# Sixteen column tiles of a mixer's input projection as 2x2 block products in a stage of their own, their results through DRAM

## The chip, the cores and the metric

The kernel runs on one core of one Trainium2 chip. The metric is the time of one execution on the device in microseconds (us). Three runs of the kernel before took 2117.59, 2117.65 and 2117.67 us; one more run was profiled, and all rows of the trace come from that one. PE is TensorE, DVE VectorE, ACT ScalarE, POOL GpSimd, and SP the engine that only issues DMAs.

## What is computed

One encoder layer for 1024 tokens of width 1024: a SwiGLU feed-forward (FFN) half step, a mixer, a second FFN half step, with a layer norm after each. Only the mixer's code changes. Its core in the reference is:

```python
proj = h @ w_in        # 1024 x 5152
na_q, na_k, na_v, g_q, g_k, g_v, g_g, dlf, dlb, gate_na, gate_gla = split(proj)
y_na  = neighborhood_attention(na_q, na_k, na_v, na_rpb) @ w_branch_na
y_gla = gla_bidirectional(g_q, g_k, g_v, g_g, dlf, dlb, ...) @ w_branch_gla
merged = sigmoid(gate_na) * y_na + sigmoid(gate_gla) * y_gla
return merged @ w_out
```

NA is neighbourhood attention with 8 heads of 64 columns on a grid of 16 rows by 64 columns; GLA is gated linear attention with 4 heads, in both directions, with silu(g_g) as its output gate. The kernel keeps float32 accuracy: every operand is split into a rounded high part and the remainder as low part (`split`, `load_w`), and each product of 128x128 weights with 512 tokens is three matmuls (high x high, high x low, low x high). Activations stand with the 1024 columns as 8 tiles `k` of 128 partitions, in two halves `h` of 512 tokens.

## The kernel before, in words

PE's instructions run in the order of the program text (`tc.manual_schedule(engines={PE})`); a scheduler orders the other engines, each of which then runs its own list strictly in order. `run` draws from generators that issue PE's dense matmuls; each step of three adds 0.65 to a clock (`STEP`). `at(t, f)` puts an event on that clock: when the dense work has come to `t`, `f` issues its instructions between two steps. `flush` issues what is left.

The stages, in order: the first FFN (`one.go`), the values of NA (`tok_major(wnv)`, stored to DRAM as `vscr`), the NA stage, the GLA stage, the merge, the output projection with its norm, the second FFN.

The FFNs compute two column tiles at a time as a 2x2 block product, seven block products in place of eight (Strassen's scheme, Winograd's form): `sums_of` makes the four sums of activation blocks (`T`), `factors` the four sums of weight blocks, `product` issues one block product (4 tiles x 3 matmuls = 12 matmuls), `blocks` strings them together.

The mixer before takes no part in that: each column tile is loaded by `load_w` and multiplied by `mm_steps`, 48 matmuls for both halves.

- NA stage (L1016 to L1026). `qk_pair(p)` computes the q and k tiles of two heads (96 matmuls), with q's moving operand read in the order of attention blocks (`blk`), and splits them from PSUM into the attention's operands on ACT and DVE (L928 to L936). Its 16 small loads `vp<-vscr` (L916) go over SP's queue. Sixteen attention events per pair run between the matmuls of the next pair: event i issues the scores of block i (2 matmuls), the transposes of block i-2 (3) and, in every second event, the values of two blocks (12). Between scores and transposes of a block stand DVE's bias add and minimum (L966), ACT's exponential (L968), DVE's reciprocal and scaling (L970, L971). `spill` computes the four tiles of GLA's q and k and stores them; `decay_rank` and `tok_major(wgv)` follow.
- GLA stage (L1223 to L1235). `gate_na(j)` computes a gate tile, its sigmoid and the NA branch's projection; `out_gate(i)` computes a tile of the output gate (48 matmuls), its silu and the product with the GLA output, which `gla_otrans` had put into DRAM (`gos`). GLA's own work is placed by `GLA_T0`, `GLA_DT` and `GLA_OUT`.
- Merge (L1243). `merge(j)` loads two weight tiles, computes a gate tile (48 matmuls), its sigmoid, the GLA branch's projection (24 matmuls), and combines both branches; then `project` multiplies by `w_out`.

Of the kernel before, what the change touches and what calls it, by code (L numbers as in the profile page):

```python
# [8 lines left out]
F32 = mybir.dt.float32  # L9
F32R = mybir.dt.float32r  # L10
# [8 lines left out]
P = 128  # L19
# [19 lines left out]
GLA_D0 = 6.0  # L39
GLA_T0 = 27.5  # L40
GLA_DT = 31.1
GLA_NEXT = 8.5
GLA_OUT = (15.0, 29.0, 29.0, 37.0)
NA_T0 = 3.3
FIRST = (1, 2, 4, 8)
# [19 lines left out]
def hybrid_layer(ctx, tc, xT, wg1, wu1, wds1, wd1, wg2, wu2, wds2, wd2, wcol, wnv, wgv, wdl, wgate,  # L65
# [362 lines left out]
    class Ffn:  # L428
# [133 lines left out]
        def blocks(self, fs):  # L562
# [4 lines left out]
            for f in [*fs, None]:  # L567
                if f is not None:
                    w = self.factors(f)
                    X = dps()  # L570
# [248 lines left out]
    one = Ffn(ffn1, x, xr, half(xT), wg1, wu1, wds1, wd1, 0)  # L819
    one.go(first, ((0, 0, HF), (1, 0, HF)), lambda h, c0, cn: to_x(x1, h))  # L820

# [4 lines left out]
    gos = dram.tile([4, P, S], F32, tag="gos", name="gos")  # L826
    m1s = dram.tile([KD, P, S], F32, tag="m1s", name="m1s")

    dls = dram.tile([32, S], F32, tag="dls", name="dls")


    def tok_major(w_d, dst, alloc=None):
        wq = []
        for i in range(4):
            if alloc is None:
                wh, wl = load_w(w_d[i], D)
                wq += [(wh[:, :HF], wl[:, :HF]), (wh[:, HF:], wl[:, HF:])]
                continue
            raw = wpool.tile([P, D], F32, tag="raw", name=nm("raw"), bufs=2)
# [19 lines left out]

    def spill(src, m, dst, scale=1.0):  # L860
        w = load_w(src, KD * m)
        for h in range(2):
            ps = dps((m, HF))
            yield from mm_steps(ps, w, x1h[h])
            sb = stage()
            nc.scalar.activation(sb[:m], ps, AF.Copy, scale=scale)
            nc.sync.dma_start(dst[:, h * HF:(h + 1) * HF], sb[:m])

    run(tok_major(wnv, lambda t: vscr[t * P:(t + 1) * P, :], one.hpair))
    assert not pending  # L870
    ffn1.close()
    x1h = [[x1[k][h] for k in range(KD)] for h in range(2)]

    def decay_rank():
# [5 lines left out]
        for h in range(2):  # L880
# [13 lines left out]
            nc.sync.dma_start(dls[:, h * HF:(h + 1) * HF], sb[0:32])  # L894

    vgrid = vscr.rearrange("(r c) e -> r c e", c=64)
    nap = ExitStack()
# [7 lines left out]
    def qk_pair(p):  # L905
        wq = load_w(wcol[p], D)
        wk = load_w(wcol[4 + p], D)
        k2 = [npool.tile([P, S], F32R, tag="k2", name=nm("k2"), bufs=4) for _ in range(2)]
# [3 lines left out]
        pair[p] = (q2, k2, kl, vp)  # L912
        for b in range(4):
            w = COLW[b]
            for g in range(4):
                nc.sync.dma_start(vp[:4 * w, 4 * b + g, :],  # L916
                                  vgrid[4 * g:4 * g + 4, COL0[b]:COL0[b] + w, p * P:(p + 1) * P])
        for h in range(2):
            hs = slice(h * HF, (h + 1) * HF)
            pq = dps()  # L920
            yield from mm_steps(pq, wq, [(blk(hi), blk(lo)) for hi, lo in x1h[h]])
            sides = []
            for hh in range(2):
                a, o = slice(64 * hh, 64 * hh + 64), slice(64 - 64 * hh, 128 - 64 * hh)
                t = npool.tile([P, HF], F32R, tag="q2", name=nm("q2"), bufs=4)
                q2[hh][h] = t
                sides.append((hh, a, o))
                nc.scalar.activation(t[a], pq[a], AF.Copy, scale=0.125)  # L928
                nc.vector.scalar_tensor_tensor(t[o], pq[a], 0.125, t[a].bitcast(F32),
                                               ALU.mult, ALU.subtract)  # L930
            pk = dps()
            yield from mm_steps(pk, wk, x1h[h])
            for hh, a, o in sides:
                nc.scalar.activation(k2[hh][a, hs], pk[a], AF.Copy)
                nc.vector.tensor_copy(k2[hh][o, hs], pk[a])
                nc.vector.tensor_tensor(kl[a, hs], pk[a], k2[hh][a, hs].bitcast(F32),  # L936
                                        ALU.subtract)


# [75 lines left out]

    run(qk_pair(0))  # L1016
    gl = [spill(wcol[8 + i], P, gqk[i], 0.125 if i < 2 else 1.0) for i in range(4)]
    na_events(0, 16, NA_T0, 41)
    run(gl[0], decay_rank(), qk_pair(1))
    na_events(16, 32, NA_T0, 41)  # L1020
    run(gl[1], gl[2], qk_pair(2))
    na_events(32, 48, NA_T0, 31)
    run(gl[3], qk_pair(3))
    na_events(48, 67, NA_T0, 41)
    run(tok_major(wgv, lambda t: gv[t]))
    flush()  # L1026
# [25 lines left out]
    for h, tag in enumerate(("on", "gst")):  # L1052
        hs = slice(h * HF, (h + 1) * HF)
        dlr = gp.tile([32, HF], F32, tag=tag, name=nm("dlr"))
        nc.sync.dma_start(dlr, dls[:, hs])
# [9 lines left out]
    def gla_decay(hd):  # L1065
# [6 lines left out]
        v = gp.tile([P, 8, P], F32, tag="gvt", name=nm("gvt"))  # L1072
        nc.sync.dma_start(v, gv[:, :, hd * P:(hd + 1) * P].rearrange("t p e -> p t e"))
# [108 lines left out]
    def gla_otrans(hd, h):  # L1182
        on = heads[hd]["on"]
        pt = aux.tile([P, HF], F32, tag="pt", name=nm("opt"), bufs=1)
        for t in range(4):
            nc.tensor.transpose(pt[:, t * P:(t + 1) * P], on[:, t], ident)
        sb = gp.tile([P, HF], F32, tag="gst", name=nm("gst"))
        nc.scalar.activation(sb, pt, AF.Copy, scale=ngt[:, 0:1])
        nc.sync.dma_start(gos[hd, :, h * HF:(h + 1) * HF], sb)

# [15 lines left out]
    def out_gate(i):  # L1206
        w = load_w(wcol[12 + i], D)
        for h in range(2):
            ps = dps()
            yield from mm_steps(ps, w, x1h[h])  # L1210
            og_in = lp.tile([P, HF], F32, tag="hr", name=nm("ld"), bufs=1)
            nc.sync.dma_start(og_in, gos[i, :, h * HF:(h + 1) * HF])
            sb = stage()
            nc.scalar.activation(sb, ps, AF.Silu)
            nc.vector.tensor_tensor(sb, sb, og_in, ALU.mult)
            hi, lo = atile(F32R), atile(F32R)
            split(sb, hi, lo)
            og[i][h] = (hi, lo)

    at(GLA_D0, lambda: gla_decay(0))  # L1220
    for hd in range(4):
# [10 lines left out]
        for i, t in enumerate(GLA_OUT):  # L1232
            add(t, (gla_out, gla_otrans)[i % 2], hd, i // 2)
    run(*[gate_na(j) for j in range(KD)], *[out_gate(i) for i in range(4)])
    assert not pending  # L1235
    gla.close()
# [6 lines left out]
    def merge(j):  # L1243
        wga = load_w(wgate[KD + j], D)
        wb = load_w(wbr[1, j], HF)
        for h in range(2):
            m1 = lp.tile([P, HF], F32, tag="hr", name=nm("ld"), bufs=1)
            nc.sync.dma_start(m1, m1s[j, :, h * HF:(h + 1) * HF])
            pg = dps()
            yield from mm_steps(pg, wga, x1h[h])  # L1250
            sb = stage()
            nc.scalar.activation(sb, pg, AF.Sigmoid)
            py = dps()
# [8 lines left out]
    def project(d, h, sink):  # L1262
# [133 lines left out]
```

## Time and profile before

| | |
|---|---|
| median of three runs | 2117.65 us |
| the profiled execution | 2116.91 us |
| its span, first to last instruction | 2115.1 us |
| mean granted clock of PE | 0.998 |
| PE busy | 2091.7 us, 99% of the span, 9818 matmuls |
| DVE, ACT, POOL busy | 1327.8, 866.7, 90.8 us |
| HBM traffic | 199.91 MB read, 82.97 MB written |

The profile is that of one core. A matmul of 512 columns is listed with a duration of some 390 ns, but the next one starts before it ends: the price of a matmul is the distance from its start to the next start, which a timeline shows, and not its listed duration. "Busy" is the union of the durations, so an engine that is busy 99% may still have waits hidden in long durations. "SPq" rows are SP's DMA issues. The chain that ended last puts 93% of the span on PE.

### The profile page before, as it was taken

How to read it: one execution, taken by the hardware profiler on the slowest of the kernel's cores; microseconds unless marked ns; L12 is line 12 of the kernel's file. 1: busy time of each engine (PE TensorE's matmuls, PEld its weight loads, DVE VectorE, ACT ScalarE, POOL GpSimd, SP SyncE). 2: the span in 40 equal slices, each digit the busy share in tenths (PEclk: the TensorE clock that was granted, in tenths of full speed). 3: DMA queues.
4: the chain of work that ended last, by engine and by line, in shares of the span. 5: the costliest groups of instructions: out<-in, count | busy, mean ns of one | idle time of the engine just before them, and what ended most of it. 6: DMA issues, size and time to landing. Idle time of an engine off the chain costs nothing.

```text
span 2115.1 us, 26389 instructions
## 1 busy us (share of the span) xinstructions
PE 2091.7 (99%) x9818; PEld 1705.1 (81%) x9818; DVE 1327.8 (63%) x2270; ACT 866.7 (41%) x1439; POOL 90.8 (4%) x86
## 2 busy tenths in 40 slices
PE   9999999999999999999999999999999999999997
PEld 7888888888887867777888888877888888888887
DVE  8667776456668244543777433499776776557647
ACT  6444444312234244445566422245544444322222
POOL 0000000000014100000000000034000000000001
PEclk9999999999999999999999999999999999999999
DMA  4444443496631223223334222221343443396722
GB/s 146 152 142 150 166 162 110 142 327 218 224 115 43 93 78 99 89 61 100 92 108 122 91 85 80 95 81 69 111 178 126 168 151 134 125 318 215 239 100 80
DMA packets 145409, 284.63 MB, mean 135 GB/s; under 512 B 15264, under 2 KB 39584, under 8 KB 145280
## 3 DMA queue, kind: packets, MB, share of 16 engines
q1 hardware_dynamic: 145280, 282.94, 39.9%
q8 instruction: 77, 1.26, 0.2%
q14 instruction: 52, 0.43, 0.1%
HBM read 199.91 MB, written 82.97 MB: 134 GB/s over the span
## 4 chain that ended last, share of the span: by engine, by line
PE 93%; DVE 4%; POOL 1%; DMA 1%; issue 1%; ACT 0%; SPq 0%; DVEq 0%; POOLq 0%; ACTq 0%
PE d L556 15%; PE d L558 15%; PE d L557 15%; PE d L119 9%; PE d L121 9%; PE d L120 9%; PE d L658 3%; PE d L657 3%; PE d L656 3%; PE d L852 1%; PE d L854 1%; PE d L853 1%; PE po L997 1%; PE pt L979 1%; PE s L962 1%
## 5 line engine op out<-in xcount | busy, mean ns | idle before, releaser
L119 PE MATMUL d<-xh,wh 128*128 128x512 f32 x640 | 259.1, 405 | 0.1
L120 PE MATMUL d<-xl,wh 128*128 128x512 f32 x640 | 251.3, 393 | 1.0 <-POOL xl L409 0.5
L121 PE MATMUL d<-xh,wl 128*128 128x512 f32 x640 | 251.2, 393 | 0.5 <-DVE wl L109 0.5
L128 ACT ACTIVATE wh<-raw 128x512 fp32r<-128x512 f32 (+4 forms) x132 | 98.0, 753 | 173.2 <-PE d L557 70.2
L129 DVE TENSOR_TENSOR wl<-raw,wh 128x512 fp32r<-128x512 f32 (+4 forms) x132 | 109.9, 841 | 88.2 <-ACT wh L128 88.1
L678 DVE TENSOR_TENSOR a<-a,d 128x512 f32<-128x512 f32 (+1 forms) x152 | 100.0, 658 | 90.1 <-PE d L558 60.0
L119 PEld LDWEIGHTS d<-xh,wh 128*128 128x128 f32 x640 | 120.3, 188 | 32.8 <-issue 4.5
L121 PEld LDWEIGHTS d<-xh,wl 128*128 128x128 f32 x640 | 120.3, 188 | 27.0 <-DVE wl L109 1.0
L120 PEld LDWEIGHTS d<-xl,wh 128*128 128x128 f32 x640 | 120.5, 188 | 26.6 <-DVE xl L129 2.0
L108 ACT ACTIVATE wh<-raw 128x512 fp32r<-128x512 f32 (+1 forms) x91 | 82.5, 907 | 136.0 <-PE d L120 80.0
L109 DVE TENSOR_TENSOR wl<-raw,wh 128x512 fp32r<-128x512 f32 (+1 forms) x91 | 96.1, 1057 | 62.9 <-ACT wh L108 62.1
L656 PE MATMUL d<-hh,wh 128*128 128x512 f32 (+1 forms) x368 | 134.5, 365 | 0.0
L658 PE MATMUL d<-hh,wl 128*128 128x512 f32 (+1 forms) x368 | 133.2, 362 | 0.0
L657 PE MATMUL d<-hl,wh 128*128 128x512 f32 (+1 forms) x368 | 133.2, 362 | 0.0
L556 PE MATMUL d<-a,wh 128*128 128x512 f32 x320 | 124.9, 390 | 1.6 <-DVE hr L584 1.6
L558 PE MATMUL d<-xh,wl 128*128 128x512 f32 x320 | 124.8, 390 | 0.4 <-DVE wl L129 0.4
L557 PE MATMUL d<-a,wh 128*128 128x512 f32 x320 | 124.7, 390 | 0.0
L558 PE MATMUL d<-a,wl 128*128 128x512 f32 x320 | 124.7, 390 | 0.0
L558 PE MATMUL d<-hh,hl 128*128 128x512 f32 x320 | 124.7, 390 | 0.0
L556 PE MATMUL d<-xh,wh 128*128 128x512 f32 x320 | 124.7, 390 | 0.0
L556 PE MATMUL d<-hh,hh 128*128 128x512 f32 x320 | 124.7, 390 | 0.0
L557 PE MATMUL d<-xl,wh 128*128 128x512 f32 x320 | 124.7, 390 | 0.0
(309 smaller groups left out, 4690.0 us busy)
## 6 DMA issues: line engine op xcount, KB each, us to landing
raw<-in_wu SPq DMA_DIRECT2D x44, 512.0 KB
raw<-in_wg SPq DMA_DIRECT2D x43, 512.0 KB
ops<-oh SPq DMA_DIRECT2D x84, 256.0 KB
ops<-ol SPq DMA_DIRECT2D x84, 256.0 KB
oh<-ops SPq DMA_DIRECT2D x48, 256.0 KB
ol<-ops SPq DMA_DIRECT2D x48, 256.0 KB
hid<-oh SPq DMA_DIRECT2D x40, 256.0 KB
hid<-ol SPq DMA_DIRECT2D x40, 256.0 KB
```

The lines of the kernel that those rows point to most:

```text
L119: nc.tensor.matmul(ps, a, xh, start=k == 0, stop=False)
L120: nc.tensor.matmul(ps, a, xl, start=False, stop=False)
L121: nc.tensor.matmul(ps, wl[:, k * m:(k + 1) * m], xh, start=False, stop=k == n - 1)
L128: nc.scalar.activation(hi, src, AF.Copy)
L129: nc.vector.tensor_tensor(lo, src, hi.bitcast(F32), ALU.subtract)
L556: nc.tensor.matmul(ps, a, xh, start=first and k == 0, stop=False, **sg)
L557: nc.tensor.matmul(ps, a, xl, start=False, stop=False, **sg)
L558: nc.tensor.matmul(ps, wl[:, k * P:(k + 1) * P], xh, start=False, stop=k == n - 1, **sg)
L656: nc.tensor.matmul(ps, wh, hi, start=k == 0, stop=False)
L657: nc.tensor.matmul(ps, wh, lo, start=False, stop=False)
L658: nc.tensor.matmul(ps, wl, hi, start=False, stop=k == n - 1)
L678: nc.vector.tensor_tensor(a, a, ps, ALU.add)
```

## The change

- Sixteen column tiles (NA's q and k, GLA's q and k, the output gate) are taken out of their places and computed as eight pairs in a new stage `pairs`, between `decay_rank` and the NA stage, with the FFN's `factors` and `product` and new `sums_of`. Each pair is 7 block products of 12 matmuls. For this the first norm's outputs are kept (`x1r`) until `sums_of` has read them.
- The results go to DRAM over GpSimd's queue (`qks`, `gqk`, `ogs`; 32 stores of 256 KB). `qk_pair` no longer multiplies: it reads q and k back over GpSimd's queue and splits them from SBUF; its 16 `vp` loads move from SP's to GpSimd's queue too, behind the first q and k loads.
- NA's 64 events now run in one go from 13.0 on the clock, 1.05 apart, between `tok_major(wgv)` and four gate tiles `gate_gla(4..7)`; before, 2.36, 2.36, 1.73 and 1.98 apart.
- `wgv`'s weights are loaded during the last pair (`last()`).
- `gate_gla(j)` computes the gate tiles of the merge earlier and stores them unsigmoided to `gts`; 1, 2 and 3 follow `gate_na`, 0 stands just ahead of the merge. `merge` loads them and applies the sigmoid.
- `gla_otrans` multiplies by the gate that `gla_out` loads from `ogs`; `out_gate` only loads and splits. The last head's output stays in SBUF.

```diff
-NA_T0 = 3.3
+NA_T0 = 13.0
+NA_DT = 1.05
+NA_GATES = (4, 5, 6, 7)
+GLA_GATES = (1, 2, 3)
...
+    def pairs(mb, items, last):
+        x, T = mb.x, mb.T
+        b11, b21, b22 = ([x[k + o][h] for k in range(4)] for o, h in ((0, 0), (4, 0), (4, 1)))
+
+        def store(out, h, t, src=None):
+            dst, fn, scale = out
+            if src is not None or fn != AF.Copy or scale != 1.0:
+                nc.scalar.activation(t, t if src is None else src, fn, scale=scale)
+            nc.gpsimd.dma_start(dst[:, h * HF:(h + 1) * HF], t)
...
+                w = mb.factors(wcol[it[0]], wcol[it[1]])
+                if it is items[-1]:
+                    last()
+                X = dps()
+                yield from mb.product(X, w["a11"], b11, True)
...
+            if prev:
+                yield from mb.product(pX, pw["a22"], T[3])
+                with hoist():
+                    store(g[3], 0, mb.tmp(), pX)
...
+    for i in range(4):
+        one.sums_of(i)
+    run(decay_rank())
...
+    run(pairs(one, [(p, 4 + p, plain(qks[p], 0.125), plain(qks[4 + p])) for p in range(4)]
+              + [(8, 9, plain(gqk[0], 0.125), plain(gqk[1], 0.125)),
+                 (10, 11, plain(gqk[2]), plain(gqk[3]))]
+              + [(12 + i, 13 + i, (ogs[i], AF.Silu, 1.0), (ogs[i + 1], AF.Silu, 1.0))
+                 for i in (0, 2)], lambda: wq.extend(tok_weights(wgv, 4))))
...
     def qk_pair(p):
-        wq = load_w(wcol[p], D)
-        wk = load_w(wcol[4 + p], D)
...
-            pq = dps()
-            yield from mm_steps(pq, wq, [(blk(hi), blk(lo)) for hi, lo in x1h[h]])
...
+            pq, pk = (npool.tile([P, HF], F32, tag="qr", name=nm("qr"), bufs=3)
+                      for _ in range(2))
+            nc.gpsimd.dma_start(pq, qks[p, :, hs])
+            nc.gpsimd.dma_start(pk, qks[4 + p, :, hs])
...
+                nc.scalar.activation(t4[a], q4[a], AF.Copy)
+                nc.vector.tensor_tensor(t4[o], q4[a], t4[a].bitcast(F32), ALU.subtract)
                 nc.scalar.activation(k2[hh][a, hs], pk[a], AF.Copy)
                 nc.vector.tensor_copy(k2[hh][o, hs], pk[a])
                 nc.vector.tensor_tensor(kl[a, hs], pk[a], k2[hh][a, hs].bitcast(F32),
                                         ALU.subtract)
+        for b in range(4):
+            w = COLW[b]
+            for g in range(4):
+                nc.gpsimd.dma_start(vp[:4 * w, 4 * b + g, :],
+                                  vgrid[4 * g:4 * g + 4, COL0[b]:COL0[b] + w, p * P:(p + 1) * P])
...
+    qk_pair(0)
+    for p in range(1, 4):
+        at(NA_T0 + (16 * p - 13) * NA_DT, lambda p=p: qk_pair(p))
+    na_events(0, 67, NA_T0, NA_T0 + 67 * NA_DT)
+    run(tok_major(wgv, lambda t: gv[t], wq=wq), *[gate_gla(j) for j in NA_GATES])
...
     def merge(j):
-        wga = load_w(wgate[KD + j], D)
...
+            m1, sb = (mp.tile([P, HF], F32, tag=t, name=nm(t), bufs=3) for t in ("m1", "sb"))
+            nc.sync.dma_start(m1, m1s[j, :, hs])
+            nc.sync.dma_start(sb, gts[j, :, hs])
+            nc.scalar.activation(sb, sb, AF.Sigmoid)
```

Before, SP's queue holds these rows where the loads for NA's first two pairs stand (`vp_6026` belongs to pair 0, `vp_6380` to pair 1; `bt` are bias tiles, `raw` weights):

```order
L916 DMA vp_6026<-vscr 128x1x128 x5
L916 DMA vp_6026<-vscr 96x1x128 x4
L952 DMA bt_6192<-in_bias 128x2x288
L952 DMA bt_6243<-in_bias 128x768
L916 DMA vp_6380<-vscr 96x1x128 x4
L916 DMA vp_6380<-vscr 128x1x128 x8
L916 DMA vp_6380<-vscr 96x1x128 x4
L107 DMA raw_6699<-in_wcol 128x1024
```

Now GpSimd's queue holds, from the last stores of the new stage on (L888), the loads of pair 0 (`qr_7282` to `qr_7299`, `vp_7281`) and then those of pair 1 (`qr_7459` and on, `vp_7458`):

```order
L888 DMA ogs<-hr_7271 128x512
L990 DMA qr_7282<-qks 128x512
L991 DMA qr_7283<-qks 128x512
L990 DMA qr_7298<-qks 128x512
L1007 DMA vp_7281<-vscr 96x1x128 x4
L1007 DMA vp_7281<-vscr 128x1x128 x2
L991 DMA qr_7299<-qks 128x512
L1007 DMA vp_7281<-vscr 128x1x128 x6
L1007 DMA vp_7281<-vscr 96x1x128 x4
L990 DMA qr_7459<-qks 128x512
L991 DMA qr_7460<-qks 128x512
L990 DMA qr_7475<-qks 128x512
```

The loads of a pair, 20 in all, now stand behind the stage's last store and behind those of the pair before, in one list; pair 1's rest and the first of pair 2 follow in the same way.

On DVE, before, pair 1's k is split from PSUM (`d_6489`) between the attention's own instructions (`e`, `sm`; `kl` and `k` are the split's results):

```order
L966 ISA e_6547,sm_6548<-s_6544,bt_6542 128x384
L966 ISA sm_6548 128x1
L935 CAST k_1310_6377<-d_6489 64x512
L970 RECIPROCAL sm_6548<-sm_6548 128x1
L936 TENSOR_TENSOR kl_6379<-d_6489,k_1310_6377 64x512
L971 TENSOR_SCALAR e_6547<-e_6547,sm_6548 128x384
L935 CAST k_1311_6378<-d_6489 64x512
L936 TENSOR_TENSOR kl_6379<-d_6489,k_1311_6378 64x512
```

Now pair 1's q and k are split from the tiles that GpSimd's queue loads (`qr_7459`, `qr_7460`, `qr_7475`), right behind the minimum of event 2 (`e_7442`) and ahead of its scaling:

```order
L1037 ISA e_7442,sm_7443<-s_7439,bt_7437 128x384
L1037 ISA sm_7443 128x1
L999 TENSOR_TENSOR q_1680_7463<-qr_7459,q_1680_7463 64x8x4x16
L1001 CAST k_1674_7455<-qr_7460 64x512
L1002 TENSOR_TENSOR kl_7457<-qr_7460,k_1674_7455 64x512
L1041 RECIPROCAL sm_7443<-sm_7443 128x1
L1001 CAST k_1675_7456<-qr_7460 64x512
L1042 TENSOR_SCALAR e_7442<-e_7442,sm_7443 128x384
L999 TENSOR_TENSOR q_1681_7469<-qr_7459,q_1681_7469 64x8x4x16
L1002 TENSOR_TENSOR kl_7457<-qr_7460,k_1675_7456 64x512
L999 TENSOR_TENSOR q_1684_7479<-qr_7475,q_1684_7479 64x8x4x16
L999 TENSOR_TENSOR q_1685_7485<-qr_7475,q_1685_7485 64x8x4x16
```

The split's first row there waits for a DMA now, where it waited for PE, and the attention rows behind it wait with it. The first row of pair 2's split stands in the same manner behind the minimum of event 6.

More of the change, by code (lines that the diff above doesn't have):

```diff
@@ L819, in hybrid_layer, with to_x1, sink @@
     one = Ffn(ffn1, x, xr, half(xT), wg1, wu1, wds1, wd1, 0)
-    one.go(first, ((0, 0, HF), (1, 0, HF)), lambda h, c0, cn: to_x(x1, h))
+    x1r = [[None, None] for _ in range(KD)]
+    def to_x1(h, c0, cn):
+        put = to_x(x1, h)
+        def sink(d, y):
+            put(d, y)
+            x1r[d][h] = y
+        return sink
+    one.go(first, ((0, 0, HF), (1, 0, HF)), to_x1)
     vscr = dram.tile([S, HF], F32, tag="vscr", name="vscr")
@@ L858, in tok_major @@
             nc.sync.dma_start(dst(t), sb)
[L860 to L871, printed above, removed]
@@ L872, in hybrid_layer @@
-    x1h = [[x1[k][h] for k in range(KD)] for h in range(2)]
+    def pairs(mb, items, last):
[6 more added lines that the diff above has]
+            nc.gpsimd.dma_start(dst[:, h * HF:(h + 1) * HF], t)
+        prev = None
+        for it in [*items, None]:
+            if it:
+                w = mb.factors(wcol[it[0]], wcol[it[1]])
[3 more added lines that the diff above has]
+                yield from mb.product(X, w["a11"], b11, True)
+                s1 = mb.tmp()
+                with hoist():
+                    nc.scalar.activation(s1, X, AF.Copy)
+                Y = dps()
+                yield from mb.product(Y, w["a12"], b21, True)
+                with hoist():
+                    nc.vector.tensor_tensor(s1, Y, s1, ALU.add)
+                store(it[2], 0, s1)
+            if prev:
+                g, pX, p5, pw = prev
+                yield from mb.product(pX, pw["s3"], T[2])
+                with hoist():
+                    nc.vector.tensor_tensor(p5, pX, p5, ALU.add)
+                store(g[3], 1, p5)
+            if it:
+                Z = dps()
+                yield from mb.product(Z, w["s1"], T[0], True)
+                s5 = mb.tmp()
+                with hoist():
+                    nc.scalar.activation(s5, Z, AF.Copy)
+                yield from mb.product(X, w["s2"], T[1])
+                s2 = mb.tmp()
+                with hoist():
+                    nc.scalar.activation(s2, X, AF.Copy)
+            if prev:
+                yield from mb.product(pX, pw["a22"], T[3])
+                with hoist():
+                    store(g[3], 0, mb.tmp(), pX)
+            if it:
+                yield from mb.product(Z, w["s4"], b22)
+                with hoist():
+                    nc.vector.tensor_tensor(s2, Z, s2, ALU.add)
+                store(it[2], 1, s2)
+                prev = it, X, s5, w
@@ L894, in decay_rank @@
             nc.sync.dma_start(dls[:, h * HF:(h + 1) * HF], sb[0:32])
+    run(tok_major(wnv, lambda t: vscr[t * P:(t + 1) * P, :], one.hpair))
+    assert not pending
+    x1h = [[x1[k][h] for k in range(KD)] for h in range(2)]
+    one.x, one.xr = x1, x1r
+    for i in range(4):
+        one.sums_of(i)
+    run(decay_rank())
+    plain = lambda t, scale=1.0: (t, AF.Copy, scale)
+    wq = []
+    run(pairs(one, [(p, 4 + p, plain(qks[p], 0.125), plain(qks[4 + p])) for p in range(4)]
[3 more added lines that the diff above has]
+                 for i in (0, 2)], lambda: wq.extend(tok_weights(wgv, 4))))
+    ffn1.close()
     vgrid = vscr.rearrange("(r c) e -> r c e", c=64)
@@ L1014, in na_events, with gate_gla @@
                 at(t, lambda i=s: na_scores(i))
[L1016 to L1025, printed above, removed]
+    def gate_gla(j):
+        w = load_w(wgate[KD + j], D)
+        for h in range(2):
+            ps = dps()
+            yield from mm_steps(ps, w, x1h[h])
+            sb = stage()
+            nc.scalar.activation(sb, ps, AF.Copy)
+            nc.sync.dma_start(gts[j, :, h * HF:(h + 1) * HF], sb)
+    qk_pair(0)
[3 more added lines that the diff above has]
+    run(tok_major(wgv, lambda t: gv[t], wq=wq), *[gate_gla(j) for j in NA_GATES])
     flush()
@@ L1206, in out_gate @@
     def out_gate(i):
-        w = load_w(wcol[12 + i], D)
         for h in range(2):
[L1209 to L1212, printed above, removed]
             sb = stage()
[L1214 to L1218, printed above, removed]
+            nc.sync.dma_start(sb, gos[i, :, h * HF:(h + 1) * HF])
+            og[i][h] = atile(F32R), atile(F32R)
+            split(sb, *og[i][h])
     at(GLA_D0, lambda: gla_decay(0))
@@ L1233, in hybrid_layer @@
             add(t, (gla_out, gla_otrans)[i % 2], hd, i // 2)
-    run(*[gate_na(j) for j in range(KD)], *[out_gate(i) for i in range(4)])
-    assert not pending
+    run(*[gate_na(j) for j in range(KD)])
+    for i in range(3):
+        at(4.0 * i, lambda i=i: out_gate(i))
+    run(*[gate_gla(j) for j in GLA_GATES])
+    flush()
     gla.close()
@@ L1271, in project @@
         sink.add(a)
+    run(gate_gla(0))
     for j in range(KD):
```

72 lines of the change are left out of this document (34 added, 38 removed).

## Prediction, made before the change was run

> **What bounds the kernel now.** I read the page first: PE is busy almost throughout.
>
> ```profile
> span 2115.1 us, 26389 instructions
> PE 2091.7 (99%) x9818; PEld 1705.1 (81%) x9818; DVE 1327.8 (63%) x2270; ACT 866.7 (41%) x1439; POOL 90.8 (4%) x86
> PE 93%; DVE 4%; POOL 1%; DMA 1%; issue 1%; ACT 0%; SPq 0%; DVEq 0%; POOLq 0%; ACTq 0%
> ```
>
> The chain in the third line says the same: 93% of the span is PE's own work, so a matmul taken away is time gained unless something else comes late in its place. What a matmul costs is read from stretches, by windows (us, then busy time and number per engine). The first is the twenty blocks of the first FFN, the second the mixer up to the merge, the third the 64 attention events, the fourth a part of the merge stage, the last the stretch just ahead of the mixer's tiles.
>
> ```profile
> 53.20:434.90 381.70, 380.92 (x1681) 315.25 (x1680) 247.49 (x377) 170.48 (x275) 0.00 (x0) 1.00 0.44 152
> 710.40:1345.40 635.00, 635.00 (x3241) 500.27 (x3241) 317.84 (x626) 286.16 (x480) 3.56 (x13) 1.00 0.30 92
> 737.00:990.00 253.00, 253.00 (x1382) 184.10 (x1380) 114.31 (x316) 114.09 (x255) 1.96 (x5) 1.00 0.25 79
> 1222.00:1345.00 123.00, 123.00 (x545) 101.91 (x544) 45.00 (x60) 31.32 (x46) 0.00 (x0) 1.00 0.26 82
> ...
> 690.00:710.00 20.00, 20.00 (x90) 16.55 (x90) 0.00 (x0) 3.56 (x7) 3.10 (x3) 1.00 0.17 66
> ```
>
> 381.7 us for 1681 matmuls is 0.227 us each, without a hole: a block product of 12 costs 2.72 us, a pair of column tiles done in blocks 84 x 0.227 = 19.1 us. The merge stage runs at the same pace (123.0/545 = 0.226). The granted clock is 1.00 throughout. In the mixer (second row) PE never stood still for 635 us; the other engines have half the time free, and that slack is what the change spends.
>
> **The matmuls removed.** Sixteen tiles of 48 matmuls are 768, eight pairs of 84 are 672: 96 fewer, 96 x 0.227 = 21.8 us. PE's list confirms the number, 9122 rows against 9218. The q tiles were dearer than that, because their moving operand was read in blocks; the timeline shows the first q product, the first k product and the next q product starting at
>
> ```profile
> 710.44 0.40 PE L119 MATMUL d<-xh,wh 128*128 128x512 f32 x1
> ...
> 716.18 0.40 PE L119 MATMUL d<-xh,wh 128*128 128x512 f32 x1
> ...
> 721.67 0.40 PE L119 MATMUL d<-xh,wh 128*128 128x512 f32 x1
> ```
>
> 5.74 us for q's 24 matmuls, 5.49 for k's. Eight q products in plain order save another 8 x 0.27 = 2.2 us. The attention's own matmuls, the gates and both branch projections stay the same in number. So 24.0 us can be gained, if no new wait appears.
>
> **The new stage.** Two rows first: one of DVE's split instructions of 512 columns (number | busy us, mean ns | idle before), and, from the chain, the end of the first FFN's blocks.
>
> ```profile
> L936 DVE TENSOR_TENSOR kl<-d,k 64x512 fp32r<-64x512 f32 x12 | 8.2, 687 | 0.2
> ...
> 431.45 0.70 DVE hr L584
> ```
>
> The stage's work per pair on DVE and ACT is less than an FFN block's, which PE passed without a hole in the first window. Two ends cost something. At its start `sums_of` needs 32 DVE instructions of 0.69 us, 22 us; DVE was idle from 690 to 710 us, while the values' matmuls run, and `decay_rank` and the first two products (7 + 5 us) come before the first product that needs the sums. The last sums must wait for buffers that the values' weights leave at 710. I take 1.0 us, with 0 and 4 as ends. At its end the last two products share a PSUM bank, and the second waits for DVE to read it, as the second row shows for the FFN; I take 1.0 us for that.
>
> **GpSimd's queue, the main cost.** Let S be the end of the last product. The first event's scores stand 13 clock units later, 20 steps of three matmuls, 20 x 3 x 0.227 = 13.6 us. An event costs PE the dense work between two events, 1.05/0.65 x 3 x 0.227 = 1.10 us, and its own matmuls: in the third window 704 of the 1382 are the events' (2 + 3 + 6 each), so (253.0 - 678 x 0.227)/64 = 1.55 us. One event every 2.65 us, against 253/64 = 3.95 before. Event 6 is due at S + 13.6 + 6 x 2.65 = S + 29.5.
>
> By then GpSimd's queue must have worked off a long list. Its terms come from these rows: a 512 KB load in the chain, two of ACT's groups, SP's issues of the `vp` loads in the timeline (start, us) and over all (least, median, most ns), and the dearest group on POOL.
>
> ```profile
> 1495.95 3.38 DMA raw<-in_wg
> ...
> L108 ACT ACTIVATE wh<-raw 128x1024 fp32r<-128x1024 f32 x11 | 11.6, 1057 | 4.4 <-PE d L120 4.3
> L857 ACT ACTIVATE sl<-d 128x512 f32<-128x512 f32 x6 | 3.5, 591 | 2.9 <-PE d L854 2.9
> ...
> 723.65 12.49 SPq L916 DMA_DIRECT2D vp<-vscr  x16
> ...
> L916 SPq DMA_DIRECT2D vp<-vscr x64: 510/616/1528, 710.6 to 886.0; - x64
> ...
> L409 POOL TENSOR_TENSOR xl<-a,xh 128x512 fp32r<-128x512 f32 x32 | 46.4, 1477 | 29.9 <-ACT xh L408 29.7
> ```
>
> The last store of the new stage waits for ACT: the conversion of a weight tile, which waits for S itself, then the silu, 1.06 + 0.59 us and some hops, S + 1.9. Behind that store stand the 20 loads of pair 0, the 20 of pair 1 and the first of pair 2; that one DVE wants right behind the minimum of event 6, and no row behind it, not even event 6's own scaling, passes it. That is 42 issues. With c the time that one takes, the last lands at S + 1.9 + 42c + 2; the 2 us is under the 3.38 us of a 512 KB load, for half the bytes. PE notices two events later, at the transposes, and the chain between takes about one event, so 2.6 us of lateness are free. The stall is 42c + 3.9 - 29.5 - 2.6 = 42c - 28.2 us. Nothing gives it back: PE's order is fixed and the stage has no slack in it.
>
> The trace of before has no DMA on GpSimd's queue, so c is bounded by neighbours. The same `vp` loads took SP a median of 0.616 us to issue, and 12.49/16 = 0.78 us each in the one row where a whole pair's stand together. The dearest instruction of 128 partitions on GpSimd itself is 1.477 us. It is the same work as SP's there, so I take that row's 0.78: stall 4.6 us. The ends are 0 (c = 0.616 or less) and 33.8 us (c = 1.477).
>
> [...]
>
> **The attention's pace.** DVE's groups in the old attention stage are these.
>
> ```profile
> L966 DVE CUSTOM_DVE_ANT_0 e<-s,bt 128x384 f32<-128x384 f32 x32 | 17.7, 555 | 28.2 <-PE s L962 28.2
> L966 DVE CUSTOM_DVE_ANT_0 e<-s,bt 128x288 f32<-128x288 f32 x30 | 13.7, 457 | 36.7 <-PE s L962 36.6
> L971 DVE TENSOR_SCALAR e<-e,sm 128x384 f32<-128x384 f32 x32 | 13.4, 420 | 1.1
> L971 DVE TENSOR_SCALAR e<-e,sm 128x288 f32<-128x288 f32 x31 | 11.5, 371 | 1.0
> L970 DVE RECIPROCAL sm<-sm 128x1 f32<-128x1 f32 x63 | 10.3, 163 | 34.9 <-ACT e L968 34.5
> L966 DVE DVE_READ_ACCUMULATOR2_ANT sm<- 128x1 f32 x62 | 5.1, 83 | 0.0
> ```
>
> DVE's work per event is 0.51 + 0.08 (L966), 0.16 (L970), 0.40 (L971); a pair's split adds 12 instructions of 0.69, or 0.52 per event, and the output's split 0.09.
>
> The sum, 1.76 of 2.65 us, leaves a third free, where before more than half was. The split comes in bursts of 8.2 us within some four events; twice or three times PE should lose about 1 us: 3.0 us, ends 0 and 8.
>
> **The merge.** DVE's groups in the old merge stage:
>
> ```profile
> L109 DVE TENSOR_TENSOR wl<-raw,wh 128x1024 fp32r<-128x1024 f32 x8 | 9.8, 1225 | 23.9 <-ACT wh L108 23.9
> L129 DVE TENSOR_TENSOR ml<-sl,mh 128x512 fp32r<-128x512 f32 x14 | 9.7, 692 | 9.1 <-ACT mh L128 9.1
> L1256 DVE TENSOR_TENSOR sl<-sl,ld 128x512 f32<-128x512 f32 x14 | 9.6, 689 | 0.3
> L1255 DVE TENSOR_TENSOR sl<-sl,d 128x512 f32<-128x512 f32 x14 | 9.6, 687 | 39.2 <-PE d L121 39.2
> L109 DVE TENSOR_TENSOR wl<-raw,wh 128x512 fp32r<-128x512 f32 x6 | 4.1, 684 | 0.0
> ```
>
> A half has 12 matmuls left, 2.72 us, where it had 36. DVE's work in it stays: multiply, add, remainder, half a weight tile, 0.69 x 3.5 = 2.41 us. SP must bring 640 KB per half, 241 GB/s, with three buffers of each kind. Gate 0's way through DRAM is covered by gate 0's own matmuls only in part. I take 2.5 us, ends 0 and 9. The gates done earlier cost PE what they cost, and SP's queue is rid of 64 small loads. The GLA stage keeps its spacing (31.0 for 31.1) and loses its output gates' DVE work: 0.
>
> **Sum.** -21.8 - 2.2 + 1.0 + 1.0 + 4.6 + 3.0 + 2.5 = -11.9 us on the profiled execution's 2116.9 (span 2115.1 and 1.8 around it): 2105.0; the median of the runs shown lies 0.7 higher: 2105.7, rounded to 2106.
>
> **Rivals.** *The queue is dear, and the kernel is slower.* Place: DVE's first split rows of pairs 1 and 2, waiting with the attention behind them for GpSimd's loads. At c = 1.06 the stall is 16.3 us, which with the other 7.5 eats the 24.0; from 1.16 on the kernel is slower by over 4 us. At 1.2 to 1.4 the stall is 22 to 31 us: 2123 to 2132. For it: nothing in the trace shows that GpSimd issues as fast as SP, and its additions take 1.48 us where DVE's take 0.69. [...] Against the rival: c = 1.16 is half as much again as SP needs for the same loads. Chance 0.21.
>
> *Nothing is gained.* [...] Chance 0.13.
>
> *The merge becomes DVE's.* The output projection's first four weight tiles (1.2 us each) must also be split there; 16 x 2.41 + 4.9 = 43.5 us is just PE's 16 x 2.72. If a half takes 3.3 us, 9 us go in place of 2.5: 2112. Chance 0.07.
>
> *The queue is cheap.* c is at most 0.65, other stalls 5 to 7.5: 2099 to 2101. Chance 0.14.
>
> That the change does not do what it says is excluded by PE's list.
>
> **Chances.** The forecast has 0.45, with 2101 to 2111 as its own range. Faster by over 0.2% (4.2 us, about what a measurement of this kernel can tell from no change) is 0.45 + 0.14 and a little of the merge's: 0.62. Same is 0.17, the case of no gain and the rest of the merge's; slower 0.21. The range takes in the cheap queue at its dear end and the dear one up to c = 1.25: 2098 to 2125, leaving out about 0.04 below and 0.13 above.
>
> **What will show it.** Right, step by step: 9722 matmuls; the new stage 152 to 156 us long at 0.227 us a matmul; POOL's queue rows some 0.8 us each; one wait of PE for the first scores or the transposes of events 3 to 8, of about 5 us in sum, none later above 2; events 2.7 us apart. Wrong: issues on GpSimd above 1 us, with DVE standing at L999 or L1001 for ten microseconds and more; PE's attention events apart by more than 3 us to the end, which would be DVE's or ACT's pace; or PE waiting in the merge for DVE at L1331 and after.

## The result, and the profile after

The changed kernel takes 2187.15 us (median of 4 runs, 2185.26 to 2189.7) against 2117.66 for the kernel before beside it: ratio 1.0325, interval 1.0308 to 1.0343. It is 3% slower, 69.5 us, and 62 us above the upper end of the range. The page's first lines of the changed kernel, and its chain of waits:

```profile
span 2185.1 us, 26639 instructions
PE 2089.6 (96%) x9722; PEld 1698.4 (78%) x9722; DVE 1395.1 (64%) x2388; ACT 904.1 (41%) x1520; POOL 162.3 (7%) x198
PE 77%; issue 10%; DVE 6%; POOL 3%; ACT 2%; DMA 2%; SPq 0%; POOLq 0%; DVEq 0%; ACTq 0%
```

The 96 matmuls are gone (9722), yet PE's busy time fell by only 2 us, and 10% of the chain is now "issue": time in which an engine waited for nothing that the profile shows. Windows show where (us, then busy time and number for PE, PEld, DVE, ACT and POOL, then granted clock, DMA share, GB/s):

```profile
714.00:871.00 157.00, 157.00 (x694) 127.75 (x693) 74.45 (x108) 63.72 (x101) 16.38 (x30) 1.00 0.33 114
...
889.50:899.50 10.00, 0.19 (x2) 0.02 (x1) 2.24 (x5) 1.17 (x3) 3.62 (x6) 0.75 0.24 76
...
907.00:927.00 20.00, 0.50 (x3) 0.08 (x2) 0.59 (x3) 1.14 (x3) 7.21 (x12) 0.61 0.25 76
...
935.00:951.00 16.00, 0.93 (x6) 0.72 (x4) 2.32 (x7) 1.33 (x3) 3.98 (x6) 0.62 0.13 37
...
970.00:1035.00 65.00, 63.31 (x366) 43.70 (x365) 36.70 (x110) 38.01 (x89) 10.41 (x16) 0.98 0.36 112
```

The new stage of pairs runs as forecast: 694 matmuls in 157 us, 0.226 each, PE never idle. Then, at the attention's first events, PE stands still for 10, 20 and 15 us, with every other engine mostly idle too, and again at 960 and 1033 us. In between (970 to 1035) it works. PE's waits in the mixer, by who released it (us in total, times, longest):

```profile
PE pt L1050 <- ACT et L1053: 19.5, 1, 19.5
PE po L1068 <- ACT et L1053: 16.1, 2, 9.7
PE pt L1050 <- DVE e L1042: 15.4, 2, 15.1
PE s L1031 <- ACT k L1000: 9.8, 1, 9.8
PE kps L1192 <- ACT ket L1194: 3.5, 3, 2.7
PE d L122 <- ACT m L1280: 3.5, 3, 1.2
```

The first four rows are 60.8 us in six waits. ACT and DVE, named there, were themselves held up: the next split rows stand in their queues ahead of the attention's. DVE's timeline has, between the minimum of event 2 and the rest of that event,

```profile
907.03 0.08 DVE L1037 DVE_READ_ACCUMULATOR2_ANT sm<- 128x1 f32 x1
926.52 0.69 DVE L999 TENSOR_TENSOR q<-qr,q 64x512 fp32r<-64x512 f32 x1 [19.41 <-ACT q L998]
...
928.33 0.15 DVE L1041 RECIPROCAL sm<-sm 128x1 f32<-128x1 f32 x1
```

Among the waits of all engines from 714 to 1140 us are

```profile
POOL vp L1007 <- issue: 114.4, 48, 5.9
...
DVE k L1001 <- DMA qr<-qks: 33.6, 3, 14.4
ACT k L1000 <- DMA qr<-qks: 32.9, 3, 13.6
...
ACT q L998 <- DMA qr<-qks: 31.4, 3, 19.5
```

The read-backs of q and k (`qr`) came late, and GpSimd, which issues them, stood 114 us at its `vp` loads without a releaser. The chain shows that at the single load (start us, us):

```profile
902.31 0.68 POOL vp L1007
902.99 2.63 issue
905.62 0.69 POOL vp L1007
906.31 2.98 issue
909.29 0.68 POOL vp L1007
909.97 2.64 issue
...
961.40 3.01 DMA qr<-qks
```

A `vp` load's own row is 0.68 us, but the next starts 3.3 to 3.7 us after it. The list of DMA issues gives the same loads' time from issue to landing:

```profile
vp<-vscr POOLq DMA_DIRECT2D x32, 64.0 KB, 3.1
```

So the next load goes out about 0.3 us after the last has landed (the one issued at 905.62 landed at 908.99, the next started at 909.29): one at a time, though each waits only for the semaphore of an issue some eight places earlier, long done (the load at 905.62 waits for one that landed at 889.50). GpSimd's timeline has the ends of the stretch that the prediction priced, from pair 0's first load to the first read-back of pair 2:

```profile
877.77 0.55 POOL L990 DMA_DIRECT2D qr<-qks  x1
...
961.40 0.59 POOL L990 DMA_DIRECT2D qr<-qks  x1
```

40 issues in 83.6 us are 2.09 us each, where the prediction took 0.78.

### The profile page after: what moved, and what is told of

It is laid out like the page before. It is cut to its first block, busy times and chain, and to the rows that moved or that the text cites. A ratio compares the mean times of both kernels' runs of the same rounds, so it can differ in the third digit from the quotient of the medians.

```text
span 2185.1 us, 26639 instructions
## 1 busy us (share of the span) xinstructions
PE 2089.6 (96%) x9722; PEld 1698.4 (78%) x9722; DVE 1395.1 (64%) x2388; ACT 904.1 (41%) x1520; POOL 162.3 (7%) x198
## 4 chain that ended last, share of the span: by engine, by line
PE 77%; issue 10%; DVE 6%; POOL 3%; ACT 2%; DMA 2%; SPq 0%; POOLq 0%; DVEq 0%; ACTq 0%
PE d L559 16%; PE d L561 15%; PE d L560 15%; PE d L122 5%; PE d L124 5%; PE d L123 4%; PE d L660 3%; PE d L661 3%; PE d L659 3%; POOL vp L1007 1%; PE po L1068 1%; PE pt L1050 1%; PE s L1033 1%; PE att L1222 1%; PE d L871 1%
## 5 line engine op out<-in xcount | busy, mean ns | idle before, releaser
L122 PE MATMUL d<-xh,wh 128*128 128x512 f32 x384 | 159.0, 414 | 3.9 <-ACT m L1280 3.5
L559 PE MATMUL d<-a,wh 128*128 128x512 f32 x384 | 149.8, 390 | 2.4 <-DVE hr L587 1.6
L123 PE MATMUL d<-xl,wh 128*128 128x512 f32 x384 | 150.9, 393 | 0.9 <-POOL xl L412 0.5
L124 PE MATMUL d<-xh,wl 128*128 128x512 f32 x384 | 151.1, 393 | 0.5 <-DVE wl L112 0.5
L561 PE MATMUL d<-xh,wl 128*128 128x512 f32 x384 | 149.5, 389 | 0.5 <-DVE wl L132 0.5
L559 PE MATMUL d<-xh,wh 128*128 128x512 f32 x384 | 149.5, 389 | 0.0
L560 PE MATMUL d<-a,wh 128*128 128x512 f32 x384 | 149.4, 389 | 0.0
L560 PE MATMUL d<-xl,wh 128*128 128x512 f32 x384 | 149.4, 389 | 0.0
L561 PE MATMUL d<-a,wl 128*128 128x512 f32 x384 | 149.4, 389 | 0.0
L559 PE MATMUL d<-hh,hh 128*128 128x512 f32 x384 | 149.4, 389 | 0.0
L560 PE MATMUL d<-hl,hh 128*128 128x512 f32 x384 | 149.4, 389 | 0.0
L561 PE MATMUL d<-hh,hl 128*128 128x512 f32 x384 | 149.4, 389 | 0.0
L131 ACT ACTIVATE hh<-sr 128x512 fp32r<-128x512 f32 x168 | 105.9, 631 | 96.1 <-DVE sr L500 34.6
L132 DVE TENSOR_TENSOR hl<-sr,hh 128x512 fp32r<-128x512 f32 x168 | 114.1, 693 | 0.8
```

Source lines behind the costliest of these rows:

```text
L122: nc.tensor.matmul(ps, a, xh, start=k == 0, stop=False)
L123: nc.tensor.matmul(ps, a, xl, start=False, stop=False)
L124: nc.tensor.matmul(ps, wl[:, k * m:(k + 1) * m], xh, start=False, stop=k == n - 1)
L131: nc.scalar.activation(hi, src, AF.Copy)
L132: nc.vector.tensor_tensor(lo, src, hi.bitcast(F32), ALU.subtract)
L559: nc.tensor.matmul(ps, a, xh, start=first and k == 0, stop=False, **sg)
```

## The experiments

**Which loads, and on which queue.** Four kernels, each an edit to the changed kernel. The kernel before stood at 2118.8 us beside them.

```
- nc.gpsimd.dma_start(vp[:4 * w, 4 * b + g, :], ...)
+ nc.sync.dma_start(vp[:4 * w, 4 * b + g, :], ...)
```

> The 64 loads of the values' tiles (vp, L1007) go to SyncE's queue; the read-back of q and k stays on GpSimd's. In the changed kernel's trace GpSimd issues the next vp load about 0.3 us after an earlier one has landed, 2.7 to 3.3 us apart, though no semaphore holds it; I take that as the whole cause (theory A). A expects the five long waits of PE from 889 to 1043 us (62 us, and the matmuls at a low granted clock around them) to go, the read-backs to be issued 0.6 us apart, and 2105 to 2115 us. Theory B: every load of GpSimd's queue is slow there, the read-backs too; then the long waits of DVE and ACT for qr stay and the time is above 2130 us. Theory C: the pace of the attention (DVE, ACT) is what fails and the queue only follows; then above 2170 us.

Measured 2126.52 us (ratio to before 1.0040, 1.0027 to 1.0053): 61 us of the 69 are back. The vp loads are the cause, not the attention's pace (theory C falls). But it lies 11.5 us above A's upper end, so A is not all.

```
- nc.gpsimd.dma_start(pq, qks[p, :, hs])
- nc.gpsimd.dma_start(pk, qks[4 + p, :, hs])
+ nc.sync.dma_start(pq, qks[p, :, hs])
+ nc.sync.dma_start(pk, qks[4 + p, :, hs])
```

This edit together with the one above:

> Both kinds of loads (vp, L1007, and q and k, L990 and L991) go to SyncE's queue; GpSimd keeps the stores. Theory A (the vp loads alone hold GpSimd's queue up): within 5 us of the run that moves vp alone, 2105 to 2115 us. Theory B (all of GpSimd's loads are slow): only here the waits go, so at least 15 us below the run that moves vp alone. Theory C (the attention's own pace): above 2170 us.

Measured 2125.58 us (ratio 1.0031, 1.0020 to 1.0042), 1 us below the run before. GpSimd's read-backs of q and k cost nothing by themselves: theory B falls.

The columns outermost, on GpSimd's queue:

```
  nc.gpsimd.dma_start(vp[:4 * w, 4 * b + g, :],
      vgrid[4 * g:4 * g + 4, COL0[b]:COL0[b] + w, p * P:(p + 1) * P]
+     .rearrange("r c e -> c r e"))
```

> The vp loads stay on GpSimd's queue, 64 of them with the same bytes in the same 512-byte pieces, but each walks its 4 rows by 24 or 32 columns of tokens with the columns outermost instead of the rows. The order of the value rows within a group of keys is then another, so the output of the attention is not the reference's; every instruction and its size stay. [...] If GpSimd's queue takes such small loads one at a time whatever their shape, or if DVE shuts GpSimd out, the rows stay 2.7 to 3.3 us apart and the time stays at 2180 to 2190 us.

Measured 2118.37 us (ratio 0.9995, 0.9985 to 1.0004), 0.4 us above the 2105 to 2118 that A expected here: 69 us come back with queue, count and bytes unchanged. What made the loads dear is their shape.

The edit of q and k alone:

> Only the 16 read-backs of q and k (L990, L991) go to SyncE's queue; the 64 vp loads stay on GpSimd's, in their order. Theory A: the vp loads still take some 2.5 us each, 40 us for a pair's 16, and the value products of an event wait for them instead of DVE's split; for four pairs the queue is still the longer chain only for the first two or three: 2140 to 2185 us. If the read-back behind the stores was what cost the time, it falls to 2105 to 2115 us.

Measured 2123.66 us (ratio 1.0023, 1.0012 to 1.0033). That is a miss for A as I wrote it, and it sharpens A. GpSimd's row shows the vp loads as slow as ever:

```profile
L1007 POOL DMA_DIRECT2D vp<-vscr x64 | 43.1, 675 | 131.1 <-issue 124.8 <-DMA qr<-qks 4.8 <-DVE sm L1041 1.4
```

125 us of unexplained waiting, and it hardly costs anything. 16 loads at about 2.7 us (0.68 and 2.0 of waiting) serve 16 events at 2.63 us: the values come nearly in time (PE's value products wait 4.6 us for them in all). Slow loads alone didn't slow the kernel by much; what did was the next pair's read-backs behind them in one queue, on which DVE and ACT wait with the attention behind them.

**The rows in order again, and the other holes.** The next four start from a form of the loads that leaves the value rows in the reference's order. Before stood at 2118.84 us beside them.

```
- for g in range(4):
-     nc.gpsimd.dma_start(vp[:4 * w, 4 * b + g, :],
-                         vgrid[4 * g:4 * g + 4, COL0[b]:COL0[b] + w, p * P:(p + 1) * P])
+ for r in range(4):
+     nc.gpsimd.dma_start(vp[r * w:r * w + w, 4 * b:4 * b + 4, :],
+                         vgrid[r::4, COL0[b]:COL0[b] + w, p * P:(p + 1) * P]
+                         .rearrange("g c e -> c g e"))
```

> The 64 vp loads are cut the other way: each brings one row of four (row r of all four groups of keys, 32 or 24 columns of tokens by 4 groups by 512 bytes) in place of one group of four rows; same queue, number of loads, bytes and pieces, and the same tile at the end, so the attention is the reference's. The outermost dimension is 32 or 24 instead of 4. [...] A rival, that the run with columns outermost was fast because its output was another or by its contiguous addresses: above 2150 us.

Measured 2119.46 us (ratio 1.0001, 0.9992 to 1.0010). Its group row, and one pair's loads in its timeline:

```profile
L1007 POOL DMA_DIRECT2D vp<-vscr x64 | 37.1, 587 | 25.9 <-PE po L1069 25.0 <-PE s L1034 0.4 <-issue 0.3
```

```profile
943.53 9.51 POOL L1007 DMA_DIRECT2D vp<-vscr  x16 [0.42 <-PE s L1034]
```

The waiting without a releaser falls from over a hundred us to 0.3, and 16 loads take 9.51 us, 0.59 each. A, which expected 2112 to 2120 us, holds in this form too, and the rival of another output or of contiguous addresses falls. With the queue as cheap as this, though, the forecast's own sum would be 2101, and the kernel only equals the one before. So other terms were wrong as well. Its PE waits in the GLA stage (1067 to 1290 us), where the prediction had "0":

```profile
PE d L122 <- ACT m L1281: 3.5, 3, 1.2
PE kps L1193 <- ACT ket L1195: 3.0, 2, 2.6
```

Before had no wait of PE there. The next two runs each change one thing.

```
- GLA_T0 = 27.0; GLA_DT = 31.0; GLA_OUT = (15.0, 28.8, 28.8, 36.0)
+ GLA_T0 = 27.5; GLA_DT = 31.1; GLA_OUT = (15.0, 29.0, 29.0, 37.0)
```

> As vp_by_rows, and the GLA stage's clock numbers set back to those of before (GLA_T0 27.5, GLA_DT 31.1, GLA_OUT 15, 29, 29, 37). In the run with columns outermost the GLA stage from the first decay product to the last transpose took 213.3 us, before 207.1: three holes of 1.6 us before a product that waits for ACT's sigmoid (L1280) and one of 3.0 us at the transposes of head 3 (L1192). If the new numbers place the sigmoid behind the three exponentials on ACT, the three holes go: 4 to 6 us below vp_by_rows. If the holes come from the output gate's new multiplication or from lines that the numbers don't touch: within 2 us.

Measured 2112.50 us (ratio 0.9969, 0.9958 to 0.9981), 7.0 below vp_by_rows, more than the 4 to 6 expected. In the run with columns outermost ACT's timeline shows the order that the new numbers had made (start, us):

```profile
1131.58 1.07 ACT L1179 ACTIVATE gkt<-gn 128x1024 f32<-128x1024 f32 x1
1133.02 1.06 ACT L1176 ACTIVATE gz<-gz 128x1024 f32<-128x1024 f32 x1 [0.37 <-DVE gz L1174]
1133.99 0.19 ACT L1178 ACTIVATE dec<-bl 128x8 f32<-128x8 f32 x1
1134.08 1.05 ACT L1181 ACTIVATE gqt<-gn 128x1024 f32<-128x1024 f32 x1
1135.15 1.28 ACT L1281 ACT_TABLE_LOAD   x1
1136.44 0.60 ACT L1281 ACTIVATE m<-d 128x512 f32<-128x512 f32 x1
```

The sigmoid of one half (`m`) comes behind the three long exponentials and a table load, and PE, which needs its PSUM bank, waits 1.2 us at each of three heads. With the old numbers these waits are gone, as is half of the wait at `kps` (3.0 to 1.5 us).

```
- at(4.0 * i, lambda i=i: out_gate(i))
+ at(14.0 + 4.0 * i, lambda i=i: out_gate(i))
```

> As vp_by_rows, with out_gate(0..2) 14 clock units later in the run of gate_gla(1..3). In the run with columns outermost ACT waits 2.6 us at 1235 us for the read-back of gos (L131) with head 3's copy of the transposed keys (L1194) queued behind it, and PE 3.0 us for that. If so, that hole goes: 2 to 4 us below vp_by_rows, unless the split now comes late for the merge (its first product then waits). If other work on ACT holds the copy: within 1 us.

Measured 2115.66 us (ratio 0.9985, 0.9976 to 0.9993), 3.8 below vp_by_rows: the wait at `kps` falls from 3.0 to 0.6 us. The output gate's split had waited on ACT for its read-back, with head 3's copy behind it.

```
- for h in range(2):
+ for what, h in (("q", 0), ("k", 0), ("k", 1), ("q", 1)):
...
```

> As vp_by_rows, but qk_pair loads and splits q's first half, k's first half, k's second half, q's second half, in this order; the first event needs both halves of k and only the first of q, and in the changed kernel k's second half stands behind six vp loads because only three buffers are there. If the holes of 5 to 6 us around the first three events (first scores, first transposes) come from that place in the queue: 3 to 6 us below vp_by_rows. If they come from the transfers themselves (7 to 9 us from issue to landing beside the weights): within 2 us.

Measured 2121.05 us (ratio 1.0007, 0.9998 to 1.0015), no gain; that it lies 1.6 above vp_by_rows is not clear of the spread. The distance to the first scores, 2.2 us in vp_by_rows, is back at a matmul's, and one of 3.7 us appears at a transpose 17 us later: these loads are late as a whole, and their order only moves the hole.

**Together, and the price of the parts.** Before stood at 2119.55 us beside these four. The two edits that had gained:

> vp_by_rows with the two edits that each gained by themselves: the GLA stage's old clock numbers (7.0 us below vp_by_rows) and out_gate(0..2) 14 units later (3.8 us below it). They take away different holes (1.6 us at each of three heads; 3.0 us at head 3, of which the old numbers had left 1.9 us): if they add up, 2119.5 - 7.0 - 2 to 3.8 = 2108 to 2111 us.

Measured 2110.83 us (ratio 0.9963, 0.9950 to 0.9975): the upper end of what was expected, 8.6 of 10.8 us add up.

```
- NA_T0 = 13.0; NA_DT = 1.05
+ NA_T0 = 16.0; NA_DT = 1.0
```

> As rows_gla_outgate, with the attention 3 clock units later and as much tighter (NA_T0 16, NA_DT 1.0, which end at 83.0 in place of 83.35). What is left at its start are holes of 3.3, 1.2, 1.5 and 1.5 us around the first events, with half-clock matmuls behind them, where the loads land 5 to 8 us after their issue. If these loads are just late, 3 units (4.6 steps of three matmuls, 3.1 us) cover them: 3 to 7 us below rows_gla_outgate. If the tighter pace then fails (events 2.57 us apart, DVE's 1.76 us in each): no gain or slower.

Measured 2106.66 us (ratio 0.9938, 0.9925 to 0.9950), 4.2 below: the first loads were late, and three units of dense work cover about half of it (PE's waits at the first events fall from 6.5 to 3.9 us, and the granted clock of the five runs is 0.995 to 0.998, where rows_gla_outgate has 0.994 to 0.995). The events stayed 2.62 us apart in the median. This is the fastest kernel of the study, 0.6% ahead of the one before.

```
- X = dps()
- yield from mb.product(X, w["a11"], b11, True)
...
+ for c, out in ((it[0], it[2]), (it[1], it[3])):
+     w = load_w(wcol[c], D)
...
+     for h in range(2):
+         ps = dps()
+         yield from mm_steps(ps, w, x1h[h])
...
+             store(out, h, mb.tmp(), ps)
...
- for i in range(4):
-     one.sums_of(i)
```

> As rows_gla_outgate, but the new stage computes its sixteen column tiles by plain products (48 matmuls each, 768 in place of 672) and needs no sums; stores, read-backs and all that follows stay. It prices the block products alone: 96 x 0.227 = 21.8 us, less what the stage's ends cost (1.0 us for the last two products that share a PSUM bank): 20 to 22 us above rows_gla_outgate. If DVE's and ACT's work for the block products costs PE time elsewhere: less than 18 us.

Measured 2129.96 us (ratio 1.0052, 1.0037 to 1.0068), 19.1 above rows_gla_outgate, just under the 20 to 22 expected: the block products are worth what their matmuls say, less the ends, within 1 us.

vp_by_rows with `nc.sync` in place of `nc.gpsimd` at the vp loads:

> As vp_by_rows, with these loads on SyncE's queue. vp_on_sp, which had the old cut there, stood at 2126.5 us, with a hole of 6.8 us at the first transposes and 10.5 us from the second event to the third. [...] If SyncE's queue is the cause, since bias loads and stores of the values stand behind 16 loads of 1.05 us each: 2124 to 2129 us as before.

Measured 2128.51 us (ratio 1.0045, 1.0031 to 1.0058), as with the old cut there (2126.52), and not the 2116 to 2121 us expected if the old cut were slow on SyncE too. The kernel's time does not gain from the cut on SyncE, though the issues do: a row of these loads is 0.65 us with the old cut and 0.40 with the new one (medians), and the first pair's sixteen, old and new, are

```profile
876.77 16.78 SPq L1007 DMA_DIRECT2D vp<-vscr  x16
...
876.58 12.20 SPq L1007 DMA_DIRECT2D vp<-vscr  x16
```

The old cut costs (16.78 - 12.20)/16 = 0.29 us per load more than the new one there, against over 2 us on GpSimd's queue (2.7 against 0.6). What holds the kernel up on SyncE is another thing. The time fits the expectation that names the biases behind the 16 loads, but no row waits for a bias in this trace. On ACT, pair 1's split stands ahead of the first events' exponentials and waits for its read-back:

```profile
900.85 1.28 ACT L1000 ACTIVATE k<-qr 64x512 fp32r<-64x512 f32 x2 [1.95 <-DMA qr<-qks]
...
904.06 0.54 ACT L1040 ACTIVATE e<-e,sm 128x288 f32<-128x288 f32 x1
```

DVE's list has the same order, and PE's wait of 9.1 us, at an early event's transposes, ends behind these rows. In vp_by_rows, pair 1's split stands behind five events' minimums on DVE. Why the scheduler ordered the lists in another way for the loads on SyncE no run shows.

## Why the prediction was wrong, step by step

**The step that failed is the price of an issue on GpSimd's queue**: "It is the same work as SP's there, so I take that row's 0.78." It was not the same work. Measured c is 2.09 us, beyond even the upper end of 1.477 that the nearest rows gave. The formula around it held: 42c - 28.2 with c = 2.09 gives 59.6 us of lateness behind pair 2's first read-back. Event 8's scores, the first behind it, start at 968.6; the stage's last matmul starts at 875.0 and S is some 0.3 us later, so S + 13.6 + 8 x 2.65 is 910.1, and they are 58.5 us late.

That PE's four groups of waits sum to 60.8 as well is in part luck: the last of them, 9.7 us at 1033, stands behind pair 3's loads, which the formula doesn't have, and up to event 8 the waits are 51.1 us, with slower matmuls between them (a granted clock of 0.65 to 0.68 from 899.5 to 907, 927 to 935 and 951 to 970 us). Nor is it one wait, as was forecast: the first is for pair 0's own k.

The place (DVE's and ACT's split rows waiting for `qr` with the attention behind them) is the one named in the rival "the queue is dear", which had 0.21 and decided from c = 1.16, and the sign of being wrong that goes with it, DVE standing at L999 or L1001 for ten microseconds and more, is what the trace shows (19.4 and 14.4 us). Its own times, 2123 to 2132, are still 55 us short, and what spoke for it was not the cause: GpSimd was not slow at an issue (a row of 0.68 us), and DVE was idle in the worst holes (busy 0.59 of the 20 us from 907 to 927). I bounded a queue's price by the length of instructions; what counted was the distance from one start to the next, and that hung on the transfer's shape. The range was too narrow because both its ends came from rows in which no load waited for another.

**DVE beside the loads.** No run shows DVE's work holding these issues up. In vp_by_rows the 64 loads average 587 ns among the attention's rows, and 16 of them take 9.51 us beside four events' scalings. The 19 of the 64 that run beside a scaling or a cast average 0.61 us, the other 45 average 0.58, and the longest is 0.76.

**The shape.** The cut alone took the 64 KB loads from 3.1 to 3.7 us apart to 0.59. The packet records in the changed kernel's trace, which the views only sum up, show how these loads differ from the 256 KB transfers on the same queue. Twenty of the loads run with no other transfer of that queue beside them: each has 16 packets of 4 KB, and at most 4 to 6 of them, by load, are under way at once. Of the stores and read-backs of 256 KB twenty-two run so: each has 64 such packets, and at most 13 to 19 are under way at once. The load issued at 905.62 moves its 64 KB from 907.06 to 908.40 with at most five; the store issued at 867.87 moves its 256 KB from 869.00 to 870.06 with up to eighteen. Why the next load waits until the one before has landed, no run shows.

**The terms that held.** The stage's 672 matmuls take 153.5 us, of 152 to 156. The block products gained 19.1 us, against 21.8 less 2.0 for the stage's ends. The events came 2.63 us apart, against 2.65, without the 3.0 us for the split's bursts. The merge had no wait of PE from 1360 to 1414 us; its 2.5 were not needed.

**The term that was left out.** "The GLA stage keeps its spacing (31.0 for 31.1) and loses its output gates' DVE work: 0." Its clock numbers cost 7.0 us and the place of out_gate 3.8, 8.6 together. Shifts of 0.1 to 1 unit, undone together, changed ACT's order at three places, which the spacing doesn't show.

**The first events.** I took 2 us from issue to landing and had no term for the loads of pair 0 themselves. The trace has for the read-backs `qr`

```profile
DMA to landing us min/median/max: 2.8/3.4/9.1
```

and the longest are the first three, 7.6 to 9.1 us, beside the weights' loads. The price is the 4.2 us that attention_later gained and the 3.9 us of waits that stay.

In sum: -19.1 for the block products as measured, -2.2 for q's plain order as forecast (no run isolates it), 67.7 for the queue (2187.15 - 2119.46), 8.6 for the GLA stage and about 8 for the first events make 63 of the 69.5 us. The other 6.5 are small holes that the profile shows and no run isolated: the last norm ahead of the stage waits 2.1 us for DVE where it waited 1.0, one of 0.7 us for POOL stands behind it, and behind the first of these (2.49 us from start to start, at 669.0) eight matmuls come 0.43 us apart in place of 0.227.

## What to carry to other kernels

Price a DMA queue by the distance between the starts of its rows, not by their length, and price it for the access pattern that will stand there: a load whose outermost dimension is 4 went out once in 2.7 us on the mean on GpSimd's queue (0.68 and 132.1/64 of waiting), the same bytes cut with 24 or 32 outermost once in 0.6. A slow queue costs little until something urgent stands behind the slow entries (with 125 us of unexplained waiting, qk_on_sp stood 4.9 us above the kernel before); ask for each load what is queued behind it. When matmuls are taken away, the stage is tighter everywhere, and the orders that were tuned for the old spacing have to be read again, on ACT too.

## What the runs showed of the hardware that was not expected

**The shape of a load on GpSimd's queue.** In the changed kernel the loads of 128 rows went one at a time; where loads of 96 rows were among them, two went out together, as in GpSimd's timeline

```profile
912.61 0.69 POOL L1007 DMA_DIRECT2D vp<-vscr  x1 [2.64 <-issue]
915.73 1.33 POOL L1007 DMA_DIRECT2D vp<-vscr  x2 [2.43 <-issue]
919.07 1.29 POOL L1007 DMA_DIRECT2D vp<-vscr  x2 [2.02 <-issue]
```

The 256 KB read-backs beside them were issued back to back at 0.6 us: it is not the bytes that are limited.

**The clock after a hole.** A hole of 2.45 us at the end of the output projection's first half is in the kernel before and in those after it. In the run with columns outermost PE's timeline (start, us) reads

```profile
1413.98 0.39 PE L124 MATMUL d<-mh,wl 128*128 128x512 f32 x1
1416.42 0.50 PE L237 MATMUL pl<-hr,ones_r 128*128 128x512 f32 x1 [2.06 <-ACT hr L230]
...
1417.48 0.63 PE L122 MATMUL d<-mh,wh 128*128 128x512 f32 x1
1417.91 0.63 PE L123 MATMUL d<-ml,wh 128*128 128x512 f32 x1
1418.33 0.63 PE L124 MATMUL d<-mh,wl 128*128 128x512 f32 x1
```

0.43 us from start to start, for 8 matmuls, 3.4 us at a granted clock of 0.51, then 0.227 again. In the kernel before, behind the same hole,

```profile
1416.78 0.39 PE L121 MATMUL d<-mh,wl 128*128 128x512 f32 x1
1419.24 0.50 PE L234 MATMUL pl<-hr,ones_r 128*128 128x512 f32 x1 [2.06 <-ACT hr L227]
1419.57 0.39 PE L119 MATMUL d<-mh,wh 128*128 128x512 f32 x1
1419.80 0.39 PE L120 MATMUL d<-ml,wh 128*128 128x512 f32 x1
```

they come 0.23 apart, at a granted clock of 1.00. Of the 14 traces, one of each kernel, nine have seven or eight such slow matmuls behind this hole and five have none; two profiles can differ by 1.6 us (8 x 0.2) for that alone. Why the same hole has slow matmuls behind it in one profile and none in another, no run shows.
